# A decoder layer's MLP: the first product in sevens for all pairs, two of each seven made early and kept in DRAM, the second product in sevens for every other pair

## The chip, the cores and the metric

The kernel runs on one core of a Trainium2 chip. The metric is the device time of one execution in microseconds (us). The core has five engines with instruction queues of their own: TensorE (PE in the profile, with its weight loads as PEld), VectorE (DVE), ScalarE (ACT), GpSimd (POOL) and SyncE (SP), whose queue here carries the DMA transfers. Each engine works through its queue in order; semaphores make one wait for another. Matmul results go to PSUM, in banks of 128 x 512 fp32; everything else lies in SBUF or in DRAM.

## The reference

One layer: attention and a recurrent mixer in parallel, merged into `h`; then a dense MLP; then a gated embedding. The change concerns the MLP. 1024 tokens, 1024 columns, 4096 hidden columns, all fp32:

```
f = rmsnorm(h, ffn_pre_norm[i])
f = jnp.square(jax.nn.relu(f @ w_ff_in[i])) @ w_ff_out[i]
h = h + rmsnorm(f, ffn_post_norm[i])
```

## The kernel before, in words

**fp32 in three matmuls.** Each fp32 operand is split into a rounded part (hi, by an ACT copy) and the rest (lo, by a DVE or POOL subtraction). `mm3` (line 289) issues hi·hi, hi·lo and lo·hi for each block of 128 rows: lines 292, 294 and 296 of the profile, 128x512 each.

**The order of the work.** A planner written in Python (`Engine`, `Loads`, `Order`) interleaves generators by estimated times; it decides in which order instructions are written. All ACT, DVE and POOL calls go through line 113 and all transfers through line 132, so the profile tells them apart by tile names. From the MLP on, SP's queue is in the order in which the code issues the transfers.

**First product.** The hidden columns are cut into 32 blocks of 128 (`j`), two to a pair `p` (NP = 16 pairs). For each block and each half of the tokens, `ff1_half` (1450) sums 8 x 3 = 24 matmuls into a fresh bank (`zbank`, 341; tile z, operands f and wh/wl), and `ff1_evac` (1454) applies ReLU and the square into `raw_h` (tile hr). That makes 64 x 24 = 1536 matmuls.

**Second product.** It goes pair by pair: 1024 tokens x 256 hidden columns times 256 x 1024 weights. As 2 x 2 blocks this takes eight block products; pairs 0 to 14 do it in seven (Strassen-Winograd), at the price of sums of operands. `operands` (1499) makes the sums on POOL (tiles sum, ws), `prep` (1530) splits them two products ahead (tile duo; ACT, DVE, POOL), `product` (1540) does 4 banks x 3 matmuls (tile bk) and adds each bank into the running totals (tile tot, DVE) while later products of a chain go on accumulating in the same four banks (tags s1 to m1). The order of the seven is MUL = (2, 1, 6, 5, 3, 7, 4). Pair 15 is done plainly with 96 matmuls (`ff2_last`, 1649; tiles lw, lh). That makes 15 x 84 + 96 = 1356 matmuls.

**How they interleave.** `ff1(j)` (1583) puts one product of the second kind, for the pair before, behind every 12 matmuls of the first. `load_w2` (1480) loads the second product's weights (w2r). `part` (1564) takes weights of later stages through the engines piece by piece: load (gp), ACT copy, DVE subtraction (gpl), two stores to DRAM (pke, pkl, pkg). The first product's weights come by `wload` (313): load (wr), ACT copy (wh), POOL subtraction (wl).

**Before the MLP,** `mixed` (1409) norms the token tiles i = 0 to 7 and `put_T` (1391) transposes and splits each into f. Tiles 0 to 3 are the first half of the tokens, 4 to 7 the second.

## Time and profile before

| | |
|---|---|
| Median of 3 runs | 1774.25 us (1773.64 to 1776.46) |
| Profiled execution, its own time | 1773.19 us |
| Its span, first to last instruction | 1771.4 us |
| Mean granted TensorE clock | 0.999 |
| PE busy | 98% |
| DVE, ACT, POOL busy | 57%, 41%, 38% |
| DMA traffic | 175.51 MB, mean 99 GB/s |

How to read the profile's lines: a group is "line, engine, operation, out<-in, shape, xcount | busy us, mean ns of one | idle of the engine just before them, and who ended it". A timeline row is start, length, engine, line, operation, and in brackets the idle before it with its releaser. A wait is "who <- for whom: us in total, times, longest". A DMA row is "out<-in, queue, xcount, KB each, us from issue to landing".

### The profile page before, as it was taken

The numbers are of one execution on the slowest core, as the hardware profiler recorded it, in microseconds if no ns is written. First come the engines' busy times: TensorE is split into PE (matmuls) and PEld (weight loads), VectorE is DVE, ScalarE is ACT, GpSimd is POOL, SyncE is SP. The second block draws the span as 40 slices with busy tenths as digits, with TensorE's granted clock in tenths as the row PEclk, the third lists the DMA queues.
The fourth block names the chain that finished last, engine by engine and source line by source line (L and its number), as shares of the span: only waits on it lengthen the run. The fifth ranks groups of instructions, "written<-read, shape, count | busy, mean of one in ns | idle before, by whom it ended". The sixth has DMA issues, their size and how long they took to land.

```text
span 1771.4 us, 25935 instructions
## 1 busy us (share of the span) xinstructions
PE 1743.8 (98%) x10192; PEld 1423.4 (80%) x10192; DVE 1017.1 (57%) x1834; ACT 732.3 (41%) x1315; POOL 670.5 (38%) x423
## 2 busy tenths in 40 slices
PE   9999989999999999999999999999999999999998
PEld 8787877878877777778888878888788888888887
DVE  6289777776534233353735466665666566556643
ACT  5824343432344343542434434343334334333454
POOL 1344131231232323332230266666665566652311
PEclk9999999999999999999999999999999999999999
DMA  4621121212332222333524132332232232305611
GB/s 163 211 95 37 49 78 47 98 43 96 86 134 84 60 60 72 110 111 135 201 96 139 64 113 95 94 115 87 92 118 91 84 95 90 123 9 179 214 48 48
DMA packets 67132, 175.51 MB, mean 99 GB/s; under 512 B 7745, under 2 KB 8129, under 8 KB 66498
## 3 DMA queue, kind: packets, MB, share of 16 engines
q1 hardware_dynamic: 67010, 173.86, 29.6%
q8 instruction: 80, 1.31, 0.3%
q14 instruction: 42, 0.34, 0.1%
HBM read 125.20 MB, written 41.94 MB: 94 GB/s over the span
## 4 chain that ended last, share of the span: by engine, by line
PE 82%; DVE 5%; DMA 5%; ACT 3%; POOL 2%; issue 2%; SPq 0%; DVEq 0%; ACTq 0%; POOLq 0%
PE z L294 18%; PE z L296 18%; PE z L292 18%; PE bk L292 6%; PE bk L294 5%; PE bk L296 5%; PE sc L275 1%; DVE xy L113 1%; PE y L275 1%; PE po L275 1%; PE pt L283 1%; PE A L275 1%; PE wr L275 1%; PE fq L275 1%; POOL wl L113 1%
## 5 line engine op out<-in xcount | busy, mean ns | idle before, releaser
L113 POOL TENSOR_TENSOR wl<-wr,wh 128x1024 fp32r<-128x1024 f32 (+1 forms) x87 | 208.0, 2392 | 431.4 <-ACT wh L113 412.2
L113 DVE TENSOR_TENSOR tot<-tot,bk 128x512 f32<-128x512 f32 x420 | 272.7, 682 | 129.9 <-PE bk L296 129.7
L292 PE MATMUL z<-uh,wh 128*128 128x512 f32 (+1 forms) x800 | 312.3, 390 | 5.5 <-ACT part L113 3.0
L296 PE MATMUL z<-uh,wl 128*128 128x512 f32 (+1 forms) x800 | 312.6, 391 | 2.7 <-POOL wl L113 2.7
L294 PE MATMUL z<-ul,wh 128*128 128x512 f32 (+1 forms) x800 | 313.6, 392 | 1.3 <-DVE ul L113 1.3
L292 PE MATMUL z<-f,wh 128*128 128x512 f32 x496 | 193.2, 389 | 0.3 <-ACT f L113 0.3
L294 PE MATMUL z<-f,wh 128*128 128x512 f32 x496 | 193.1, 389 | 0.2 <-DVE f L113 0.2
L296 PE MATMUL z<-f,wl 128*128 128x512 f32 x496 | 193.0, 389 | 0.0
L292 PEld LDWEIGHTS z<-uh,wh 128*128 128x128 f32 x800 | 151.1, 189 | 36.2 <-ACT part L113 3.5
L296 PEld LDWEIGHTS z<-uh,wl 128*128 128x128 f32 x800 | 151.0, 189 | 34.1 <-POOL wl L113 4.0
L294 PEld LDWEIGHTS z<-ul,wh 128*128 128x128 f32 x800 | 151.2, 189 | 32.3 <-issue 3.6
L292 PE MATMUL bk<-duo 128*128 128x512 f32 x420 | 164.3, 391 | 4.0 <-DVE tot L113 3.9
L294 PE MATMUL bk<-duo 128*128 128x512 f32 x420 | 163.5, 389 | 0.0
L296 PE MATMUL bk<-duo 128*128 128x512 f32 x420 | 163.5, 389 | 0.0
L113 ACT ACTIVATE wh<-wr 128x1024 fp32r<-128x1024 f32 (+1 forms) x87 | 90.3, 1038 | 119.0 <-PE z L294 89.8
L113 POOL TENSOR_TENSOR duo<-w2r,duo 128x512 fp32r<-128x512 f32 x45 | 66.7, 1483 | 166.0 <-ACT duo L113 166.0
L113 POOL TENSOR_TENSOR duo<-ws,duo 128x512 fp32r<-128x512 f32 x60 | 81.0, 1350 | 122.3 <-ACT duo L113 119.0
L292 PEld LDWEIGHTS z<-f,wh 128*128 128x128 f32 x496 | 93.1, 188 | 20.0 <-ACT f L113 0.5
L294 PEld LDWEIGHTS z<-f,wh 128*128 128x128 f32 x496 | 93.1, 188 | 19.8 <-DVE f L113 0.5
L296 PEld LDWEIGHTS z<-f,wl 128*128 128x128 f32 x496 | 93.1, 188 | 19.2
L292 PEld LDWEIGHTS bk<-duo 128*128 128x128 f32 x420 | 78.8, 188 | 23.7 <-DVE tot L113 7.0
L296 PEld LDWEIGHTS bk<-duo 128*128 128x128 f32 x420 | 78.8, 188 | 16.4
(312 smaller groups left out, 3203.5 us busy)
## 6 DMA issues: line engine op xcount, KB each, us to landing
wr<-in_wz_dram SPq DMA_DIRECT2D x48, 512.0 KB, 3.7
wr<-in_wff_dram SPq DMA_DIRECT2D x31, 512.0 KB, 3.6
w2r<-in_w_ff_dram SPq DMA_DIRECT2D x30, 512.0 KB, 4.2
xt<-in_x_dram SPq DMA_DIRECT2D x16, 512.0 KB, 4.3
gscr<-gst SPq DMA_DIRECT2D x32, 256.0 KB, 2.0
g<-gscr SPq DMA_DIRECT2D x16, 512.0 KB, 4.2
wpg<-pkg SPq DMA_DIRECT2D x16, 512.0 KB, 6.7
sw<-qk SPq DMA_DIRECT2D x48, 128.0 KB, 2.3
```

The source lines that it names most:

```text
L113: return f(*a, **kw)
L275: PE.matmul(out_, a, b, start=start, stop=stop)
L283: PE.transpose(out_, a, ident if idn is None else idn)
L292: PE.matmul(ps, ah, bh, start=start and i == 0, stop=False, skip_group_check=not start)
L294: PE.matmul(ps, ah, bl, start=False, stop=False, skip_group_check=not start)
L296: PE.matmul(ps, al, bh, start=False, stop=i == n - 1, skip_group_check=not start)
```

## The change

**First product in sevens.** Per pair it is now a 2 x 2 block product too: the input columns in two halves times the pair's two blocks of 128, and the two token halves. `put_f` takes the place of `put_T` and builds seven operands F[1] to F[7]; those that need the second half of the tokens get sums on DVE and POOL at tiles 4 to 7. Each product is 12 matmuls: 84 per pair, 16 x 84 = 1344 in all. Products 1 and 2 need only the first half of the tokens: `early` makes them for all 16 pairs (32 products, 384 matmuls) while tiles 4 to 7 are still normed, and stores them to DRAM (p1scr, cscr). The other five (SEQ = 6, 7, 4, 5, 3) are made by `first`, which `chunks` cuts into pieces of three matmuls; `take` loads the early results into `raw_h`, three times product 1 and once the finished block. After each of the five, DVE adds the bank into a block of `raw_h`. Products 6, 7, 4 accumulate in one bank, 5 and 3 in another.

**Second product.** Even pairs keep their sevens (`seven`; 8 x 84), odd pairs are done plainly (`plain`; 7 x 96), pair 15 as before (96): 1440 matmuls. The weight sums of an even pair p are made by `w2_sums` during the plain phase of pair p − 1, split, stored to DRAM (bs) and loaded again by `prep`. Some SBUF areas (tags) are assigned anew; `rooms` says which tags hold the operands of a phase, and `w2_sums` stages its splits in two of them.

```diff
+    def put_f(srcs, i):
+        ts = slice((i % 4) * 128, (i % 4) * 128 + 128)
+        if i == 4:
+            for n, p, h in ((3, 0, 0), (7, 1, 0), (5, 0, 1), (6, 1, 1)):
+                t = mtile("hl"[p], h, [128, 2, 4, 512], "f", F32R)
+                F[n] = t[:, 0], t[:, 1]
+            F[4] = [rtile([128, 4, 512], "f", tag, F32R) for tag in ("AR0", "AR1")]
...
+        G.tensor_tensor(c, c, at(1, 0), OP.subtract)
+        G.tensor_tensor(c, c, at(1, 1), OP.subtract)
+        G.tensor_tensor(t4, at(2, 0), t2, OP.subtract)
+        G.tensor_tensor(t4, t4, at(2, 1), OP.add)
+        for n, x, eng in ((7, d, V), (6, t2, V), (5, c, G), (4, t4, G)):
+            S.activation(at(n, 0), x, AF.Copy)
+            eng.tensor_tensor(at(n, 1), x, at(n, 0), OP.subtract)
...
-    def ff1_half(ps, hi, lo, h):
-        return mm3(ps, [(hi[:, k * 128:(k + 1) * 128], lo[:, k * 128:(k + 1) * 128],
-                         fT[0][h][:, k, slice(0, 512)], fT[1][h][:, k, slice(0, 512)]) for k in range(KT)])
-    def ff1_evac(ps, j, h):
-        p, x = j // 2, 2 * (j % 2) + h
-        if p not in raw_h:
...
+    SEQ = (6, 7, 4, 5, 3)
+    A_, W1, w1 = {}, {}, []
+    p1_scr, c_scr = ([dram.tile([128, 512], F32, name=f"{n}scr{p}") for p in range(NP)] for n in ("p1", "c"))
+    bs_scr = {(p, i): dram.tile([128, 2, 512], F32, name=f"bs{p}_{i}") for p in range(0, NP - 1, 2) for i in (6, 5, 7, 4)}
...
+    prods = []
+    for p in range(0, NP, 2):
+        prods += [(p, 1), (p + 1, 1), (p, 2), (p + 1, 2)]
+    NA = len(prods)
+    prods += [(p, i) for p in range(NP) for i in SEQ]
+    def a_raw(k):
+        if k < NA:
+            p, i = prods[k]
+            SY.dma_start(A_["raw"][:, k % 4], quarter(p, i - 1))
+    def w1_split(k):
+        if k >= len(prods):
+            return
+        p, i = prods[k]
+        src = A_["raw"][:, k % 4] if k < NA else W1[{6: "s2", 7: "21", 4: "22", 5: "s1", 3: "12"}[i]]
+        w = w1[k % 3]
+        S.activation(w[:, 0], src, AF.Copy)
+        (V if k < NA and k % 4 == 3 else G).tensor_tensor(w[:, 1], src, w[:, 0], OP.subtract)
...
+    def w1_mm(k, ps, start):
+        w, f = w1[k % 3], F[prods[k][1]]
+        return mm3(ps, [(w[:, 0, c * 128:c * 128 + 128], w[:, 1, c * 128:c * 128 + 128], f[0][:, c, :], f[1][:, c, :])
+                        for c in range(4)], start)
+    def early(k):
+        p, i = prods[k]
+        a_raw(k + 4)
+        w1_split(k + 2)
+        if k == 0:
+            A_["out"] = rtile([128, 4, 512], "pa", "UV")
+        if i == 1:
+            A_[p] = bank()
+        ps = A_[p]
+        yield from w1_mm(k, ps, i == 1)
+        dst = A_["out"][:, k % 4]
+        if i == 1:
+            S.activation(dst, ps, AF.Copy)
+        else:
+            S.activation(dst, ps, AF.Relu)
+            S.activation(dst, dst, AF.Square)
+        SY.dma_start((p1_scr if i == 1 else c_scr)[p], dst)
...
+    def first(k):
+        p, i = prods[k]
+        n = SEQ.index(i)
+        if n in (3, 4):
+            w1_sum(p + 1, n - 1)
+        w1_split(k + 2)
+        if n == 2:
+            w1_sum(p + 1, 1)
+        if n == 0:
+            w1_sum(p, 4)
+            w1_raw(p + 1, "21", "11")
+        if n == 1:
+            w1_raw(p + 1, "22")
+        if n == 3:
+            w1_raw(p + 1, "12")
+        if n in (0, 3):
+            W1["ps"] = zbank()
+        ps = W1["ps"]
+        yield from w1_mm(k, ps, n in (0, 3))
+        x = raw_h[p][:, {6: 1, 7: 3, 4: 2, 5: 3, 3: 1}[i]]
+        V.tensor_tensor(x, x, ps, OP.add)
+        if i in (4, 5, 3):
+            S.activation(x, x, AF.Relu)
+            S.activation(x, x, AF.Square)
...
+    def chunks(n):
+        while Y["n"] < n:
+            if Y["g"] is None:
+                Y["g"] = first(Y["k"])
+                Y["k"] += 1
+            for _ in range(3):
+                yield next(Y["g"])
+            Y["n"] += 1
+            if Y["n"] % 4 == 0:
+                for _ in Y["g"]:
+                    pass
+                Y["g"] = None
+    def take(p):
+        if p < NP:
             raw_h[p] = rtile([128, 4, 512], "hr", ("BK", "UV")[p % 2])
-        f1 = rtile([128, 512], "f1", "gst")
-        S.activation(f1, ps, AF.Relu)
-        S.activation(raw_h[p][:, x], f1, AF.Square)
-        if x == 3 and p == NP - 1:
-            last_split(1, (1,), ())
+            for x, src in ((1, p1_scr), (3, p1_scr), (2, p1_scr), (0, c_scr)):
+                SY.dma_start(raw_h[p][:, x], src[p])
+    def mlp():
+        last["turn"] = tc.manual_schedule(engines={mybir.EngineType.SP})
+        last["turn"].__enter__()
+        while sch.t < t_f.get(3, 1e9):
+            yield 0.0
+        for k in range(NA):
+            beside(k)
+            yield from early(k)
+        while sch.t < t_f.get(7, 1e9):
+            yield 0.0
+        yield from chunks(16)
+        take(1)
+        yield from chunks(20)
+        prep(0)
+        prep(1)
+        for p in range(1, NP):
+            Y["n"] = 0
+            e = p - 1
+            if e % 2 == 0:
+                for x in range(7):
+                    yield from chunks((20 * x + 20 + 3) // 7)
+                    yield from seven(items.index((e, x)))
+                    if x == 0:
+                        load_w2(p)
+                    if x == 4:
+                        take(p + 1)
+                    if p == NP - 1:
+                        if x in (1, 2, 5):
+                            e_weights((1, 2, 5).index(x))
+                        if x == 5:
+                            last_split(0, (0,), (0,))
+                            last_split(1, (0, 1), (1,))
+                continue
+            for u in range(8):
+                yield from chunks((20 * u + 20 + 3) // 8)
+                if u == 0:
+                    load_w2(p)
+                yield from plain(items.index((e, u // 2)), u % 2)
+                if u == 1:
+                    take(p + 1)
+                if 0 < u < 6 + 1:
+                    w2_sums(p, u - 1)
+                part(2 * p - 4 + u // 2, u % 2)
...
+    def rooms(e):
+        r = (("Ep", "En"), ("a", "px"), ("kk", "v"))
+        return (r[1], r[0], r[2]) if e // 2 % 2 else r
...
+        x = n - 1 - (n > 3)
+        d = split2((t2, t1, t1, t2)[x], rooms(p)[1][x % 2], G)
+        SY.dma_start(bs_scr[p, (6, 5, 7, 4)[x]], d.bitcast(F32))
...
-        a, b = operands(p, i)
-        duo[n] = (split2(a, ("Ep", "En", "a")[n % 3], V),
-                  split2(b, ("kk", "MP", "px")[n % 3], G))
+        e, x = items[n]
+        if e % 2 == 0:
+            i, room = MUL[x], rooms(e)[x % 3]
+            a = split2(operand(e, i), room[0], G)
+            if i in (2, 1, 3):
+                b = split2(w_blocks(e)[{2: 2, 1: 0, 3: 3}[i]], room[1], G)
+            else:
+                b = rtile([128, 2, 512], "duo", room[1], F32R)
+                SY.dma_start(b.bitcast(F32), bs_scr[e, i])
+            duo[n] = a, b
+            return
+        m, c = x // 2, x % 2
+        if c == 0:
+            room = rooms(e - 1)[1 + m]
+            duo[e, m] = [split2(raw_h[e][:, 2 * j + m], room[j], V) for j in range(2)]
+        if m == 0:
+            if c == 0:
+                ops["w"] = [rtile([128, 2, 1024], "ws", t, F32R) for t in ("BT", "BK2")]
+            hi, lo = ops["w"]
+            for j in range(2):
+                o = (slice(None), j, halves[c])
+                S.activation(hi[o], raw_w[e][j][:, halves[c]], AF.Copy)
+                G.tensor_tensor(lo[o], raw_w[e][j][:, halves[c]], hi[o], OP.subtract)
+    XB = ("s1", "s2", "s3", "m0", "m1")
...
+    def plain(n, part):
+        e, x = items[n]
+        if part == 0:
+            prep(n + 2)
+        m, c = x // 2, x % 2
+        a, (hi, lo) = duo[e, m], ops["w"]
+        for t in (2 * part, 2 * part + 1):
+            ts = slice(t * 128, t * 128 + 128)
+            ps = bank(XB)
+            yield from mm3(ps, [(a[j][:, 0, ts], a[j][:, 1, ts], hi[:, j, halves[c]], lo[:, j, halves[c]])
+                                for j in range(2)])
+            V.tensor_tensor(tot[m][c][:, t], tot[m][c][:, t], ps, OP.add)
...
+    def part(u, x):
+        if u >= 2 * len(GP):
             return
         dst, k, src = GP[u // 2]
         c = halves[u % 2]
         if x == 0:
-            gp["t"] = rtile([128, 2, 512], "gp", "v", F32R)
-            SY.dma_start(gp["t"][:, 0].bitcast(F32), src[:, c] if len(src.shape) == 2 else src[:, u % 2])
+            gp["t"] = rtile([128, 512], "gp", "gst")
+            SY.dma_start(gp["t"], src[:, c] if len(src.shape) == 2 else src[:, u % 2])
             return
-        raw, hi = gp["t"][:, 0].bitcast(F32), gp["t"][:, 1]
-        lo = rtile([128, 512], "gpl", "yc", F32R)
+        raw, hi = gp["t"], rtile([128, 512], "gph", "gst", F32R)
+        lo = raw.bitcast(F32R)
         S.activation(hi, raw, AF.Copy)
         V.tensor_tensor(lo, raw, hi, OP.subtract)
         SY.dma_start(dst[:, k, 0, c], hi.bitcast(F32))
         SY.dma_start(dst[:, k, 1, c], lo.bitcast(F32))
...
-    def ff1(j):
-        def body(hi, lo):
-            p = j // 2
-            if j == 3:
-                last["turn"] = tc.manual_schedule(engines={mybir.EngineType.SP})
-                last["turn"].__enter__()
-            muls = iter(range(7 * p - 7 + 4 * (j % 2), 7 * p - 7 + (7 if j % 2 else 4)))
-            for h in range(0 if j > 2 else 1, 2):
-                ps = zbank()
-                g = ff1_half(ps, hi, lo, h)
-                for k in range(2):
-                    for _ in range(12):
-                        yield next(g)
-                    if k:
-                        for _ in g:
-                            pass
-                        ff1_evac(ps, j, h)
-                    for n in [x for _ in range(1 if j > 2 else 2) for x in (next(muls, None),) if x is not None]:
-                        yield from product(n)
-                        part(n)
-                        if n % 7 == 1:
-                            load_w2(n // 7 + 1)
-                        if n in E_LOADS:
-                            e_weights(E_LOADS.index(n))
-                        if n == 7 * NP - 10:
-                            last_split(0, (0, 1), (0,))
-                        if n == 7 * NP - 9:
-                            last_split(1, (0,), (1,))
-        sch.add(body, lambda: wload(wff1[j]) if j > 2 else third())
```

In the new order, PE comes to this place in the even phase of pair 4: the boundary from product 6 (operands f_8509, weights wh_8379) to product 7 (f_8507, wh_8380), both in the bank z_10575.

```order
L292 MATMUL z_10575<-f_8509,wh_8379 128x512
L294 MATMUL z_10575<-f_8509,wh_8379 128x512
L296 MATMUL z_10575<-f_8509,wh_8379 128x512
L292 MATMUL z_10575<-f_8507,wh_8380 128x512 [waits DVE_49,Activation_49]
L294 MATMUL z_10575<-f_8507,wh_8380 128x512
L296 MATMUL z_10575<-f_8507,wh_8380 128x512 [waits Pool_49]
```

Here product 7 follows product 6 on the bank with nothing between them, and waits for DVE. On the same engine before, a first-product bank (z_12027, operands f10 and f11) ends and a second-product bank (bk_11999, product with operands duo_11996) goes on:

```order
L292 MATMUL z_12027<-f10_8329,wh_11788 128x512
L294 MATMUL z_12027<-f11_8330,wh_11788 128x512
L296 MATMUL z_12027<-f10_8329,wl_11789 128x512
L292 MATMUL bk_11999<-duo_11996,duo_11993 128x512 [waits DVE_49,Activation_49]
L294 MATMUL bk_11999<-duo_11996,duo_11993 128x512 [waits Pool_49]
L296 MATMUL bk_11999<-duo_11996,duo_11993 128x512
```

There other matmuls stood between a bank's uses; now a bank is used again at once.

SP's queue at the start of the even phase of pair 4: bs4_6, bs4_5, bs4_7 and bs4_4 are the four stored weight sums, duo_10592 is the third product's weight operand, gp and gph a piece of a later weight, pke its place in DRAM.

```order
L132 DMA bs4_4_655<-duo_10531 128x1024 [waits DMAHW2_49,Pool_49]
L132 DMA gp_10535<-in_pT_dram 128x512 [waits DMAHW4_49,DMAHW0_49]
L132 DMA pke_118<-gph_10565 128x512 [waits Activation_49]
L132 DMA pke_118<-gp_10535 128x512 [waits DMAHW5_49,DVE_49]
L132 DMA wr_8382<-in_wff1_dram 128x512 [waits DMAHW6_49]
L132 DMA wr_8382<-in_wff1_dram 128x512 [waits DMAHW7_49]
L132 DMA duo_10592<-bs4_6_652 128x1024 [waits PE_49]
```

The load that PE needs (the last row) has moved into a queue behind a store that waits for POOL and two that wait for ACT and DVE. ACT's own queue at the same place (duo_10531 is the staged sum, duo_10674 the next operand, in the buffer that the store above reads):

```order
L113 ACTIVATE duo_10531<-sum_10349 128x512 [waits PE_49]
L113 ACTIVATE duo_10671<-sum_10669 128x512 [waits DVE_49]
L113 ACTIVATE wh_8380<-wr_8383 128x512 [waits PE_49,Pool_49]
L113 ACTIVATE duo_10674<-w2r_10287 128x512 [waits DMAHW2_49,Pool_49]
L113 ACTIVATE gph_10565<-gp_10535 128x512 [waits DMAHW3_49,DMAHW1_49]
```

The copy of the staged sum waits for PE, and the later weight's copy gph stands behind an operand that waits for the store. In the kernel before, none of these steps was there: weight sums stayed on chip, and SP's queue held only loads of weights and stores of `part`:

```order
L132 DMA wr_11926<-in_wff1_dram 128x1024 [waits DMAHW2_49,Pool_49]
L132 DMA pkg_117<-gp_11909 128x512
L132 DMA pkg_117<-gpl_12019 128x512 [waits DMAHW4_49,DVE_49]
L132 DMA w2r_12024<-in_w_ff2_dram 128x1024 [waits Pool_49]
L132 DMA w2r_12024<-in_w_ff2_dram 128x1024 [waits DMAHW6_49]
```

So operands of second products came from an engine in SBUF, and come now in part from DRAM.

More of the change, by code (lines that the diff above doesn't have):

```diff
@@ L1380, in layer @@
     gn = {}
-    fT = [[None, None], [None, None]]
+    F = {}
     def ss2(srcs, jks):
@@ new lines, in w1_raw @@
+    def w1_raw(p, *names):
+        for n in names:
+            if p < NP:
+                SY.dma_start(W1[n], quarter(p, ("11", "12", "21", "22").index(n)))
+    prods = []
[15 more added lines that the diff above has]
+        (V if k < NA and k % 4 == 3 else G).tensor_tensor(w[:, 1], src, w[:, 0], OP.subtract)
@@ L1464, in last_split, with mlp_ahead @@
+    def mlp_ahead(x):
+        if x == 0:
+            w1_tiles()
+            for k in range(4):
+                a_raw(k)
+        else:
+            w1_split(0)
+            w1_split(1)
     def last_split(k, hs, ws):
@@ L1538, in layer, with seven @@
+    XB = ("s1", "s2", "s3", "m0", "m1")
     chain = [None] * 4
-    def product(n):
-        p, i = n // 7, MUL[n % 7]
+    def seven(n):
+        p, x = items[n]
+        i = MUL[x]
         prep(n + 2)
@@ L1683, in last_weights @@
     def last_weights():
-        pg = pieces(GA, "wpg", F32R)
-        P["wpg"] = [[Split(pg[4 * p:4 * p + 4]), mtile("hl"[p], 0, [128, KT, 512], "wpg", F32R)]
-                    for p in range(2)]
+        P["wpg"] = [[mtile("hl"[p], 1 - c, [128, KT, 512], "wpg", F32R) for c in range(2)] for p in range(2)]
         P["g3"] = rtile([128, D], "g3", "v")
@@ L1813, in layer @@
         out_1(i)
-    ff1_first()
-    for j in range(2, 2 * NP):
-        ff1(j)
+    sch.add(mlp)
     for i in range(8):
```

197 lines of the change are left out of this document (104 added, 93 removed).

## The prediction, made before the changed kernel had run

> **What bounds the kernel now.** I read the list of cores first, then the page's busy times and its chain, then the windows by stage, the groups by shape, the waits and last the timeline.
>
> ```profile
> core 0: 1771.4 us, clock 0.999
> PE 1743.8 (98%) x10192; PEld 1423.4 (80%) x10192; DVE 1017.1 (57%) x1834; ACT 732.3 (41%) x1315; POOL 670.5 (38%) x423
> PE 82%; DVE 5%; DMA 5%; ACT 3%; POOL 2%; issue 2%; SPq 0%; DVEq 0%; ACTq 0%; POOLq 0%
> ```
>
> TensorE is busy in 98% of the span at full clock, and 82% of the chain that ended last are matmuls. The MLP lies between about 1000 and 1640 us; in the windows (span, then PE, PEld, DVE, ACT, POOL busy, clock, DMA share, GB/s) that stretch is this row:
>
> ```profile
> 1000.00:1640.00 640.00, 635.49 (x2802) 523.40 (x2801) 385.66 (x572) 247.02 (x409) 379.75 (x252) 1.00 0.30 97
> ```
>
> PE idles 4.5 of 640 us there, POOL is busy 59%, DVE 60%, ACT 39%, and the DMA engines are at 30%. So only matmuls count, as long as none of them waits. Their spacing comes from two starts, eleven matmuls apart:
>
> ```profile
> 1013.42 0.39 PE L292 MATMUL z<-f,w 128*128 128x512 f32 x1
> 1015.92 0.39 PE L296 MATMUL z<-f,w 128*128 128x512 f32 x1
> ```
>
> (1015.92 − 1013.42) / 11 = 0.227 us each; the 0.39 shown is one matmul's own length, which overlaps the next. And PE waits for almost nobody; these are the two largest entries of the waits on PE, whole program (total, times, longest):
>
> ```profile
> PE bk L292 <- DVE tot L113: 4.2, 5, 1.7
> PE z L292 <- ACT part L113: 3.0, 1, 3.0
> ```
>
> No transfer stands in that list inside the MLP: every product today works on operands that an engine made on chip long before.
>
> **Part by part.**
>
> *Matmuls.* Of the first product 64 × 24 = 1536 matmuls become 16 × 84 = 1344; of the second 15 × 84 + 96 = 1356 become 8 × 84 + 8 × 96 = 1440. Net −108, × 0.227 = **−24.5 us**, all on PE, which is the path. That is the whole gain.
>
> *A bank that is read between two products.* Of the five later products of a pair, 6, 7 and 4 share one PSUM bank and 5, 3 another. After each, DVE adds the bank into a stored sum, and the next product goes on accumulating in that same bank. So its first matmul cannot start before that add has read the bank. The places are 6→7, 7→4 and 5→3: three per pair, 48 in all. In the new order the matmul that waits stands directly behind the last one that DVE waits for: a round trip with nothing of PE's inside. Before, each half of a column block had a bank of its own. The trip's price is in the timeline: a last matmul and the DVE add released by it, then a DVE group and the PE matmul that it released, with the next start.
>
> ```profile
> 1147.40 0.39 PE L296 MATMUL bk<-duo 128*128 128x512 f32 x1
> 1147.83 2.73 DVE L113 TENSOR_TENSOR tot<-tot,bk 128x512 f32<-128x512 f32 x4 [0.23 <-PE bk L296]
> 1020.86 1.88 DVE L113 COPY tot<-bk 128x512 f32<-128x512 f32 x3
> 1021.60 0.50 PE L292 MATMUL bk<-duo 128*128 128x512 f32 x1 [1.21 <-DVE tot L113]
> 1021.93 0.39 PE L294 MATMUL bk<-duo 128*128 128x512 f32 x1
> ```
>
> 0.39 until the matmul's end, 0.04 to DVE's start, 2.73/4 = 0.68 for the add, about 0.05 back to PE (the first of the three copies ends near 1021.5, PE starts at 1021.60), less the 0.227 that would pass anyway: 0.93. After such a wait the next start follows after 0.33 instead of 0.227, so +0.10: 1.03 us. × 48 = 49. At the 5→3 boundaries of the eight odd pairs, two DVE subtractions for operands stand in DVE's queue between PE's end and the add:
>
> ```profile
> L113 DVE TENSOR_TENSOR duo<-hr,duo 128x512 fp32r<-128x512 f32 x45 | 40.6, 901 | 0.4 <-ACT duo L113 0.4
> L113 DVE TENSOR_TENSOR gpl<-gp 128x512 fp32r<-128x512 f32 x28 | 25.6, 916 | 62.5 <-ACT gp L113 62.4
> ```
>
> Part of 2 × 0.90 shows, I take 1.2: + 8 × 1.2 = 10. **+59 us.** Lower end 48 × 0.93 = 45. Upper end: all of the 1.8 shows, 8 × 0.6 = 5 more, and the split of a later weight (the second row) sits in DVE's queue too and waits for ACT and a load, 62.5/28 = 2.2 us each today; one boundary in each of eight pairs behind one such wait is 18: 59 + 5 + 18 = 82.
>
> *Weight sums that go through DRAM.* The weight sums of an even pair are made in the odd phase before it, stored, and loaded again as operands. The last of the four sums is staged in the buffer that product number two of the even pair still reads. From there the new order gives one chain, in each of the seven even phases that an odd one precedes:
>
> 1. the last matmul of the second product ends; ACT's copy of the sum;
> 2. POOL's subtraction; SP's store, in whose queue everything later stands;
> 3. ACT's copy of the next operand, into the buffer that the store must have left;
> 4. behind it on ACT the copy of a later weight, then DVE's subtraction of it;
> 5. SP, held by these two, issues their stores, two loads of first-product weights and, as the fifth, the load of the sum that the third product needs;
> 6. the load lands; PE goes on.
>
> The rows that price it:
>
> ```profile
> L113 ACT ACTIVATE duo<-ws 128x512 fp32r<-128x512 f32 x60 | 37.2, 620 | 54.7 <-PE bk L296 53.2 <-POOL ws L113 1.5
> L113 POOL TENSOR_TENSOR duo<-ws,duo 128x512 fp32r<-128x512 f32 x60 | 81.0, 1350 | 122.3 <-ACT duo L113 119.0 <-PE bk L296 3.2
> L113 ACT ACTIVATE gp<-gp 128x512 fp32r<-128x512 f32 x28 | 17.7, 631 | 81.0 <-DMA gp<-in_w_pleg_dram 45.1 <-DMA gp<-in_w_ple_dram 11.9 <-DMA gp<-in_w_ff_dram 11.4
> bvscr<-a SPq DMA_DIRECT2D x4, 512.0 KB, 2.8
> w2r<-in_w_ff_dram SPq DMA_DIRECT2D x30, 512.0 KB, 4.2
> gscr<-gst SPq DMA_DIRECT2D x32, 256.0 KB, 2.0
> wpg<-pkg SPq DMA_DIRECT2D x16, 512.0 KB, 6.7
> 1137.27 0.43 SPq L132 DMA_DIRECT2D pke<-gp  x1
> 1137.78 0.38 SPq L132 DMA_DIRECT2D pke<-gpl  x1
> ```
>
> 0.62 (ACT) + 1.35 (POOL) + 2.8 (a 512 KB store; `bvscr<-a` is the only row of that kind) + 0.62 + 0.63 (ACT: an operand, a later weight) + 0.92 (DVE, quoted above) + 1.5 (four issues at about 0.4 before the load's own) + 4.2 (a 512 KB load) = 12.6 us. PE has meanwhile nine matmuls, 9 × 0.227 = 2.0, and one of the boundaries above, 1.0. So PE stands for 9.6 us, × 7 = **+67 us**. Low: the store at 2.0 (`gscr<-gst`, half its size) and 1.1 off for steps that overlap: 7.7 × 7 = 54. High: the load at 6.7 and the store 2.8 longer when transfers crowd: 14.9 × 7 = 104. Nothing in before covers this, and a gain is excluded, since a wait for a buffer cannot shorten anything.
>
> *The loads behind it.* The next sum is loaded behind another 1.8 MB on SP's queue and wanted 1.2 products later. What the DMA engines can carry is in one row:
>
> ```profile
> 15.00:20.00 5.00, 5.00 (x45) 5.00 (x45) 3.96 (x8) 2.33 (x6) 0.12 (x1) 1.00 1.04 393
> ```
>
> 1.8 MB at 393 GB/s is 4.6 us after the first load, against 21 matmuls, 4.8 us: nearly covered. I take 1 us × 7 = **+7** (0 to 21: from all covered to 3 us each).
>
> *The start.* For the second half of the tokens, twelve POOL and DVE sums and splits per token tile are added, while the early products want weight splits from POOL as well. Where PE comes to wait for POOL, I price the place at one POOL step, the 1.35 quoted above; I count some seven, 9.5, less the 4.5 of idle that the MLP has today (its places are gone): **+5** (0 to 10). The last pair's weights are loaded later by one queue position per phase: **+1.5** (0 to 3).
>
> *The clock.* The only stretch at the end without matmuls:
>
> ```profile
> 1765.00:1771.40 6.40, 0.00 (x0) 0.00 (x0) 3.17 (x9) 1.27 (x6) 0.72 (x1) 0.88 0.22 82
> ```
>
> The granted clock is 0.88 over 6.4 us without a matmul: about a quarter of it, 1.5 us, at half speed. An idle of 9.6 us exceeds that, so the clock will have fallen when PE resumes, and the first matmuls take up to twice as long. How long it stays low no row of before shows; a stretch of matmuls as long as the fall took to come, 6.4 − 1.5 = 4.9 us, bounds the loss at 4.9/2 = 2.4 per stall, 17 in all. Taken: half, **+8** (0 to 17).
>
> [...]
>
> *POOL as the bound.* It takes on more sums and splits; its steps last between these two:
>
> ```profile
> L113 POOL TENSOR_TENSOR ws<-w2r 128x512 f32<-128x512 f32 x30 | 47.0, 1569 | 11.2 <-PE tp L283 5.5 <-DMA w2r<-in_w_ff_dram 3.0 <-PE bk L296 0.8
> L113 POOL TENSOR_TENSOR sum<-sum,hr 128x512 f32<-128x512 f32 x15 | 19.3, 1289 | 1.2
> ```
>
> One even and one odd phase together have 84 + 96 + 120 = 300 matmuls, 300 × 0.227 = 68 us, and about 40 POOL steps by the order, 40 × 1.4 = 56 us (63 at 1.57). POOL comes closer to PE but stays under it: 0.
>
> Sum on the profiled execution. It took 1773.2 us, span 1771.4, and is 1.06 below the median, 1774.25. 1773.2 − 24.5 + 59 + 67 + 7 + 5 + 1.5 + 8 = 1896; beside the median 1897.
>
> **The rivals.**
>
> *The chain is covered.* If the store and the copies of step 4 are out of the way in time, because the engines get to them earlier than the wait for the buffer lets me believe, PE sees only the boundaries: 1773.2 − 24.5 + 59 + 5 + 1 = 1814. For it: DMA is at 30%. Against it: the wait on the second product is written into the instruction, and all after it is in order. 0.10.
>
> *The boundaries are covered.* If the accumulation need not wait for the add, as today's PE waits on DVE (4.2 us, 5 times) might suggest, only the chain is left: 1897 − 59 = 1838. Against it: today 9 to 21 other matmuls lie between a bank's last matmul and its next. 0.05.
>
> *Not slower.* This is one mechanism: semaphore waits that were long satisfied when PE reaches them. A wait in the order names only the engine. If each of those at the boundaries and at the loads is for an earlier step of that engine, PE streams on and the 108 matmuls are the whole of it: 1774.25 − 24.5 + 5 = 1755. It decides as soon as the new waits cost less than 24.5 in sum, which is 0.5 us per boundary with no stall at the loads. Against it: the add reads the very bank that the next matmul writes. 0.03.
>
> *Worse than my bounds:* 0.02, with one more stall of the chain's kind that I did not find.
>
> **How the numbers follow.** The forecast has 0.80; its time is the sum, 1897. Its own range from the lower ends: 1774.25 − 24.5 + 45 + 54 = 1849, and from the upper ends 1774.25 − 24.5 + 82 + 104 + 21 + 10 + 3 + 17 = 1987. Not all terms go one way together: I cut the top to 1960, since the two large ones share transfers only in part, and take in the second rival at 1838 below. Range 1836 to 1960. What can be told from no change is 0.2%, 3.5 us. All cases but "not slower" lie above that: slower 0.96, faster 0.03, same 0.01 (the "not slower" case with its waits only partly there).
>
> **What would show it.** Right: about 2784 matmuls of 128x512 in the two products; in the waits PE on first-product matmuls for DVE, about 48 times and 1 us each; PE on second-product matmuls for a DMA of the stored sums, seven times near 10 us; seven dips in the clock; PE's share down to about 92%. The steps fail one by one if the boundary waits are rare or longer than 1.5 us, or if the stalls for the loads are under 5 or over 15 us. The whole is wrong if PE is still busy in 97% of the span, or if the time is under 1800.

## The result, and the profile after

The changed kernel takes 1981.29 us, the median of four runs (1977.88 to 1983.99), against 1775.36 us for the kernel before beside it (four runs, 1773.64 to 1778.71): a ratio of 1.1156, 95% interval 1.1129 to 1.1184. It is slower, as forecast, but by 206 us and not by the 123 of the forecast (1897 − 1774.25), and outside the range, whose top was 1960. The profiled execution took 1983.99 us with a span of 1982.2. These are the lines of the changed kernel that answer to the first ones of before: from the list of cores,

```profile
core 0: 1982.2 us, clock 0.959
```

and from the page the busy times and the clock in 40 slices.

```profile
PE 1780.9 (90%) x10084; PEld 1430.5 (72%) x10084; DVE 1043.7 (53%) x1801; ACT 765.0 (39%) x1377; POOL 753.8 (38%) x530
...
PEclk9999999999999999999989998889898989898999
```

PE has 108 matmuls fewer, as said (10192 − 10084), but its busy time rose, from 1743.8 to 1780.9 us. That splits the 210.8 us between the spans (1982.2 − 1771.4) exactly: −24.5 for the 108 matmuls; + 61.6 because the others kept PE busy longer (1780.9 − 1743.8 + 24.5); + 173.7 of idle (1982.2 − 1780.9 = 201.3, against 1771.4 − 1743.8 = 27.6). The waits on PE say whom the idle is for:

```profile
PE bk L292 <- DMA duo<-bs: 77.2, 7, 11.8
PE z L292 <- DVE hr L113: 77.2, 48, 6.3
PE bk L292 <- ACT pa L113: 8.8, 4, 5.1
PE bk L296 <- DVE wh L113: 4.5, 2, 4.0
...
PE bk L296 <- POOL wh L113: 1.8, 1, 1.8
```

The two predicted waits stand on top, seven and 48 times, at the places that were named; the other rows shown are waits of the early products. This is the chain through DRAM at the even phase of pair 4, in the timeline of the changed kernel:

```profile
1322.93 1.15 ACT L113 ACTIVATE duo<-sum 128x512 fp32r<-128x512 f32 x2 [4.71 <-PE bk L296]
...
1323.64 2.52 POOL L113 TENSOR_TENSOR duo<-sum,duo 128x512 fp32r<-128x512 f32 x2 [3.33 <-ACT duo L113]
...
1324.95 0.32 SPq L132 DMA_DIRECT2D bs<-duo  x1
...
1327.90 0.63 ACT L113 ACTIVATE duo<-w2r 128x512 fp32r<-128x512 f32 x1 [3.15 <-DMA bs<-duo]
1328.52 0.63 ACT L113 ACTIVATE gph<-gp 128x512 fp32r<-128x512 f32 x1
...
1329.18 1.24 DVE L113 TENSOR_TENSOR gp<-gp,gph 128x512 fp32r<-128x512 f32 x1 [4.20 <-ACT gph L113]
1330.45 0.32 SPq L132 DMA_DIRECT2D pke<-gp  x1
1330.83 0.97 SPq L132 DMA_DIRECT2D wr<-in_wff_dram  x2
1331.84 0.43 SPq L132 DMA_DIRECT2D duo<-bs  x1
...
1337.73 0.77 PE L292 MATMUL bk<-duo 128*128 128x512 f32 x1 [11.66 <-DMA duo<-bs]
```

Each step is there in the order of the prediction: the copy after PE, POOL, the store, ACT freed by the store (3.15 us of waiting), the later weight, its stores, two loads, and only then the load that PE needs. PE goes on 5.9 us after that load's issue (1337.73 − 1331.84), with 277 GB/s passing at the time (below), where the sum had 4.2; in six of the seven phases it is 5.1 to 6.1 us, in the last 3.8. The last row's 0.77 shows what comes next. Windows of the same place (span, then PE, PEld, DVE, ACT, POOL busy, clock, DMA share, GB/s):

```profile
1328.00:1330.00 2.00, 0.00 (x0) 0.00 (x0) 0.82 (x1) 1.15 (x2) 1.27 (x1) 0.96 0.01 4
1330.00:1336.00 6.00, 0.00 (x0) 0.00 (x0) 0.42 (x1) 0.00 (x0) 0.00 (x0) 0.50 0.87 277
...
1338.00:1340.00 2.00, 2.00 (x6) 1.54 (x6) 0.62 (x1) 1.11 (x2) 0.41 (x1) 0.50 1.05 411
1340.00:1342.00 2.00, 2.00 (x6) 1.63 (x5) 0.82 (x3) 1.19 (x3) 2.00 (x2) 0.50 0.21 83
1342.00:1344.00 2.00, 2.00 (x7) 1.54 (x7) 1.32 (x2) 0.63 (x1) 2.00 (x3) 0.63 0.00 0
1344.00:1346.00 2.00, 2.00 (x11) 1.62 (x10) 0.50 (x1) 0.00 (x0) 2.00 (x3) 1.00 0.87 311
```

The clock falls just before 1330, some 3.8 us after the last matmul, and stays at 0.50 until about 1343.4, that is for 5.7 us after PE has resumed: six or seven matmuls in 2 us, where the full-rate window in the last row has eleven records. By the lengths of the matmuls in the timeline the half rate lasts 2.7 to 5.7 us behind the seven stalls (6 to 13 matmuls); this is the longest.

Of the 48 boundaries, the shortest waits are like the last row here. The first two rows are a long one of another kind, at the 5→3 boundary of an odd pair; the rows between are a long one of an odd phase, with what led up to it:

```profile
1254.70 3.13 DVE L113 TENSOR_TENSOR duo<-hr,duo 128x512 fp32r<-128x512 f32 x2
...
1258.48 0.80 PE L292 MATMUL z<-f,wh 128*128 128x512 f32 x1 [3.18 <-DVE hr L113]
...
1377.98 0.63 ACT L113 ACTIVATE duo<-sum 128x512 fp32r<-128x512 f32 x1 [8.45 <-DMA bs<-duo]
...
1379.90 0.63 ACT L113 ACTIVATE gph<-gp 128x512 fp32r<-128x512 f32 x1 [1.29 <-DMA gp<-in_w_ff_dram]
...
1380.56 0.69 DVE L113 TENSOR_TENSOR gp<-gp,gph 128x512 fp32r<-128x512 f32 x1 [5.29 <-ACT gph L113]
...
1381.17 1.28 DVE L113 TENSOR_TENSOR tot<-tot,bk 128x512 f32<-128x512 f32 x2
...
1382.36 0.68 DVE L113 TENSOR_TENSOR hr<-hr,z 128x512 f32<-128x512 f32 x1
...
1383.19 0.47 PE L292 MATMUL z<-f,wh 128*128 128x512 f32 x1 [3.89 <-DVE hr L113]
...
1399.55 0.47 PE L292 MATMUL z<-f,wh 128*128 128x512 f32 x1 [0.87 <-DVE hr L113]
```

A wait of 0.87 is the bare round trip of the prediction: 0.87 + 0.39 − 0.227 = 1.03 us lost. The prediction had 0.93 for this and reached 1.03 only with 0.10 for the slow restart, which comes on top here too (the next two starts follow after 0.30 and 0.24 instead of 0.227: 0.09), so the trip costs 1.12. The difference is the way back from DVE to PE, 0.15 us (an add that starts at 1324.29 and takes 0.69 lets PE go at 1325.13) and not 0.05.

All 48 at 0.87 would be 41.8 us of idle. The timeline of DVE ahead of each longer wait sorts the other 35.4 (77.2 − 41.8): 17.9 at nine boundaries behind the later weight's subtraction, as in the middle rows (three of the nine have one subtraction for an operand in front as well); 11.4 at the eight 5→3 boundaries behind the two subtractions for operands, as in the first two; 5.7 at two boundaries of the first even phase, one of them 6.26 us long, where DVE's own sums wait for POOL; 0.3 in small change. In the middle rows ACT stands for a store of an earlier staged sum, the later weight's copy stands behind it on ACT, DVE's subtraction behind that, and behind DVE's subtraction the two totals and the add that PE waits for.

### The profile page after: what moved, and what is told of

Same layout as the page of the kernel before. It is cut to its first block, busy times and chain, and to the rows that moved or that the text cites. A ratio compares the mean times of both kernels' runs of the same rounds, so it can differ in the third digit from the quotient of the medians.

```text
span 1982.2 us, 26323 instructions
## 1 busy us (share of the span) xinstructions
PE 1780.9 (90%) x10084; PEld 1430.5 (72%) x10084; DVE 1043.7 (53%) x1801; ACT 765.0 (39%) x1377; POOL 753.8 (38%) x530
## 3 DMA queue, kind: packets, MB, share of 16 engines
q8 instruction: 79, 1.29, 0.3%
## 4 chain that ended last, share of the span: by engine, by line
PE 64%; DVE 12%; DMA 10%; ACT 5%; POOL 4%; issue 3%; SPq 1%; DVEq 0%; ACTq 0%; POOLq 0%
PE z L292 12%; PE z L296 12%; PE z L294 12%; PE bk L292 5%; PE bk L296 5%; PE bk L294 5%; DVE tot L113 2%; DMA duo<-bs 2%; SPq L132 1%; DMA g<-gscr 1%; DVE duo L113 1%; DMA gp<-in_w_pleg_dram 1%; DVE hr L113 1%; DMA bs<-duo 1%; DMA pkg<-gph 1%
## 5 line engine op out<-in xcount | busy, mean ns | idle before, releaser
L113 DVE TENSOR_TENSOR tot<-tot,bk 128x512 f32<-128x512 f32 x336 | 226.4, 686 | 219.0 <-PE bk L296 218.5
L113 POOL TENSOR_TENSOR wl<-wr,wh 128x1024 fp32r<-128x1024 f32 (+1 forms) x56 | 132.5, 2368 | 420.4 <-ACT wh L113 401.2
L292 PE MATMUL bk<-duo 128*128 128x512 f32 x224 | 98.0, 437 | 77.2 <-DMA duo<-bs 77.2
L292 PE MATMUL z<-f,wh 128*128 128x512 f32 x212 | 87.8, 414 | 52.7 <-DVE hr L113 52.7
L113 ACT ACTIVATE wh<-wr 128x1024 fp32r<-128x1024 f32 (+2 forms) x89 | 78.1, 878 | 138.2 <-PE z L294 103.8
L113 POOL TENSOR_TENSOR duo<-sum,duo 128x512 fp32r<-128x512 f32 x64 | 84.6, 1331 | 87.7 <-ACT duo L113 87.7
L292 PEld LDWEIGHTS bk<-duo 128*128 128x128 f32 x224 | 47.8, 213 | 90.6 <-issue 80.1
L113 ACT ACTIVATE duo<-sum 128x512 fp32r<-128x512 f32 x64 | 38.9, 628 | 157.2 <-PE bk L296 72.5
L294 PE MATMUL bk<-duo 128*128 128x512 f32 x224 | 95.6, 427 | 0.0
L296 PE MATMUL bk<-duo 128*128 128x512 f32 x224 | 95.0, 424 | 0.0
L292 PEld LDWEIGHTS z<-f,wh 128*128 128x128 f32 x212 | 40.8, 192 | 73.2 <-ACT wh L113 20.7
L292 PE MATMUL bk<-ws,duo 128*128 128x512 f32 x224 | 89.5, 400 | 0.0
L294 PE MATMUL bk<-ws,duo 128*128 128x512 f32 x224 | 88.7, 396 | 0.0
L296 PE MATMUL bk<-ws,duo 128*128 128x512 f32 x224 | 88.5, 395 | 0.0
L296 PE MATMUL z<-f,wh 128*128 128x512 f32 x212 | 84.8, 400 | 0.0
L294 PE MATMUL z<-f,wh 128*128 128x512 f32 x212 | 84.6, 399 | 0.0
```

The lines of the kernel that those rows point to most:

```text
L113: return f(*a, **kw)
L292: PE.matmul(ps, ah, bh, start=start and i == 0, stop=False, skip_group_check=not start)
L294: PE.matmul(ps, ah, bl, start=False, stop=False, skip_group_check=not start)
L296: PE.matmul(ps, al, bh, start=False, stop=i == n - 1, skip_group_check=not start)
```

## The experiments

Theories: (A) the boundaries, the chain, the start and the clock each cost what PE is seen to wait there, and removing one removes its time; (B) something wider is the bound (transfers, POOL or DVE as a whole), and a wait that is removed comes back elsewhere.

**1. The weight sums a step earlier.** They are made ahead of the plain product of the same step, not behind it.

```diff
+                if 0 < u < 6 + 1:
+                    w2_sums(p, u - 1)
                 yield from plain(items.index((e, u // 2)), u % 2)
...
-                if 0 < u < 6 + 1:
-                    w2_sums(p, u - 1)
```

> The weight sums of an even pair are made ahead of the plain product of the same step, so the last one's staging no longer waits for the second product of the next phase; nothing else changes. Stall theory: the seven waits of PE for the stored sums (77.2 us) go, and with them the half-rate matmuls behind each, about 13 x 0.2 = 2.6 us, 18 us in all: about 1981 - 77 - 18 = 1886 us; the 48 waits for DVE stay near 77 us. Rival (crowded transfers: the loads of the sums are slow because 242 MB pass instead of 175): the loads still come late, PE still waits 3 us or more at each, and the time stays above 1930.

1899.05 us (two runs, 1896.28 to 1901.82; ratio to before 1.0662 to 1.0725): 82 us less than the changed kernel, not 95. No wait for the stored sums is left, so the loads are quick enough when their chain is gone, and crowded transfers are not the cause. Its largest waits on PE:

```profile
PE z L292 <- DVE hr L113: 77.7, 47, 7.5
PE bk L292 <- ACT pa L113: 9.1, 4, 5.2
```

**2. A bank for each of the five products.** The sums between them go through SBUF.

```diff
-        if n in (0, 3):
-            W1["ps"] = zbank()
-        ps = W1["ps"]
-        yield from w1_mm(k, ps, n in (0, 3))
-        x = raw_h[p][:, {6: 1, 7: 3, 4: 2, 5: 3, 3: 1}[i]]
-        V.tensor_tensor(x, x, ps, OP.add)
+        ps = zbank()
+        yield from w1_mm(k, ps, True)
+        h = raw_h[p]
+        x = h[:, {6: 1, 7: 3, 4: 2, 5: 3, 3: 1}[i]]
+        V.tensor_tensor(x, h[:, {6: 1, 7: 1, 4: 3, 5: 3, 3: 1}[i]], ps, OP.add)
+        if i == 5:
+            V.tensor_tensor(h[:, 1], h[:, 1], ps, OP.add)
...
-            for x, src in ((1, p1_scr), (3, p1_scr), (2, p1_scr), (0, c_scr)):
+            for x, src in ((1, p1_scr), (0, c_scr)):
```

> Each of the five later products gets a bank of its own; the sums between them are made by DVE in SBUF (one more DVE add per pair, two loads fewer). The chain through DRAM stays. Stall theory: the 48 waits for DVE (77.2 us idle, 85 us against the pace) go, the seven waits for stored sums stay near 11 us each, dips of the clock stay only behind those: about 1981 - 85 - 15 = 1881 us. Rival (DVE is the bound in the plain phases, since later weights' splits and waits for stores block its queue): the waits move to the first-product banks or the totals and at least 30 us of them stay, time above 1910.

1891.66 us (two runs, 1890.92 to 1892.40; 1.0625 to 1.0678): 90 us less. No boundary wait is left and DVE's long queue delays nobody; the stalls of the chain are a little longer, since the boundary ahead of each of the seven is gone and PE gets there earlier (7 × 1.12 = 8, an estimate):

```profile
PE bk L292 <- DMA duo<-bs: 85.7, 7, 13.3
PE bk L292 <- ACT pa L113: 8.8, 4, 5.1
PE bk L292 <- issue: 6.4, 1, 6.4
```

**3. Both.**

> Both edits together. Stall theory: only the matmuls' own saving of 24.5 us and the waits at the start (about 20 us with their clock) are left, against 7.6 us of idle that the kernel before has there: 1775 - 24.5 + 20 - 7 = about 1764 us, clock above 0.99. Rival (DMA traffic or POOL as a new bound): PE waits elsewhere for more than 25 us in sum and the time stays at or above 1780.

1805.84 us (four runs, 1801.96 to 1809.26; 1.0144 to 1.0199). The two edits add up: 93 us for the banks on top of the first edit, 86 for the sums on top of the second. But the stall theory's 1764 is missed by 42 us. Time and waits are on the rival's side (PE idles 62.5 us, 1801.9 − 1739.4, against 27.6 before), yet transfers or POOL as the bound is not what the odd and even phases show: they run nearly without waits, clock 0.99. And still the kernel is 30 us slower than before. Its windows, and that of the kernel before for the first stretch:

```profile
980.00:1110.00 130.00, 109.45 (x449) 85.34 (x449) 52.91 (x59) 66.37 (x130) 85.89 (x61) 0.92 0.48 168
1110.00:1640.00 530.00, 517.92 (x2256) 423.69 (x2256) 356.32 (x505) 210.96 (x361) 401.71 (x300) 0.99 0.51 179
```

```profile
980.00:1110.00 130.00, 127.68 (x570) 104.18 (x569) 76.21 (x119) 52.62 (x95) 73.09 (x49) 1.00 0.26 88
```

In the 130 us of the early products PE does 449 matmuls on record, before it did 570. The 121 missing ones are 121 × 0.227 = 27 us of lost time: the start, for which the prediction had 5.

**4. Matmuls that nobody reads, in the stalls of the changed kernel.** F[3] is an operand of the first product, the bank is a free one.

```diff
+                    if x == 2 and e > 0:
+                        keep = zbank()
+                        for _ in range(48):
+                            PE.matmul(keep, F[3][0][:, 0, 0:128], F[3][0][:, 0, :], start=True, stop=True)
                     yield from seven(items.index((e, x)))
```

> 48 matmuls of 128x512 whose result nobody reads (extra work, 10.9 us of PE time) are put in front of the third product of each even phase with a stall, into a free bank; all waits stay as they are. Clock theory: PE idles hardly at all in those seven places, so the clock holds and the matmuls behind run at full rate: each stall costs what it did, but the half rate behind it, about 2.6 us, goes: 1981 - 18 = about 1963 us or a little more if the filler outlasts a stall. Rival (slow matmuls come from contention with the transfers of that place): the fillers and the matmuls behind them are slow as well, the clock is no different, and the time is 1981 or above.

1985.91 us (two runs, 1983.65 to 1988.17), against 1981.29: nothing gained, a miss. The clock did hold, 0.976 instead of 0.959 over the whole, and the matmuls behind a filled stall run at full rate: from the seven stalls to the next boundary waits none takes over 0.55 us, where the changed kernel has 70. The same place as above:

```profile
1326.47 11.05 PE L1640 MATMUL z<-f 128*128 128x512 f32 x48
1338.86 0.47 PE L292 MATMUL bk<-duo 128*128 128x512 f32 x1 [1.34 <-DMA duo<-bs]
...
1356.12 0.80 PE L292 MATMUL z<-f,wh 128*128 128x512 f32 x1 [3.75 <-DVE hr L113]
```

```profile
1337.73 0.77 PE L292 MATMUL bk<-duo 128*128 128x512 f32 x1 [11.66 <-DMA duo<-bs]
...
1355.19 0.50 PE L292 MATMUL z<-f,wh 128*128 128x512 f32 x1 [1.56 <-DVE hr L113]
```

The second fence is the changed kernel. From the stall's end to the end of the next boundary wait it is 17.3 us with the filler and 17.5 without (1356.12 − 1338.86, 1355.19 − 1337.73): what PE won by its clock it waited away at the boundary, 3.75 instead of 1.56 us, since that end is set by DVE's queue. And that longer wait drops the clock in its turn: seven matmuls behind the 3.75 us take over 0.55 us, none behind the 1.56. Over all seven places this is a part of the answer: from resuming to the end of the next boundary wait PE needs 119.3 us in sum instead of 124.3, so 5 us are kept; but the stalls with the filler in them last 85.3 us in sum instead of 80.0, counted from the start of the last matmul of the kernel ahead to that of the first behind, and that takes the 5 us back. Why they last longer is not shown.

**5. The later weights' subtraction on POOL,** on top of the first edit.

```diff
-        V.tensor_tensor(lo, raw, hi, OP.subtract)
+        G.tensor_tensor(lo, raw, hi, OP.subtract)
```

> On top of the sums made earlier (the kernel of about 1899 us): the subtraction of each later weight's piece runs on POOL instead of DVE. Theory: about 36 of the 77.7 us that PE waits for DVE at the 47 or 48 boundaries come from DVE being held behind that subtraction, which waits for ACT, a load and a store; then the waits fall towards 47 x 0.87 = 41 us plus some 10 for the plain operands' splits, the half-rate matmuls behind them mostly go (10 us), and the time is about 1899 - 27 - 10 = 1862 us. Rival (the plain operands' splits on DVE make the excess): waits stay above 65 us, time above 1890.

1873.03 us (two runs, 1872.15 to 1873.90): 26 us less, where 37 were expected. The boundary waits fall by 14 us, though not as far as 51, and PE's busy time by 22 (1774.1 to 1752.0), since fewer matmuls run at half rate (granted clock 0.986 instead of 0.975; in the last 420 us 26 matmuls over 0.55 us instead of 48); a part of both comes back as idle elsewhere:

```profile
PE z L292 <- DVE hr L113: 63.7, 45, 7.4
```

So that subtraction in DVE's queue is one cause of the long boundaries and worth 26 us. The longer waits that are left stand, by the timeline, behind the two subtractions for operands, behind DVE's sums of hr that wait for POOL, and in the first even phase (7.39 us); no run takes these out one by one.

**6. The start, first attempt,** on top of both edits: an own bank for the early second product, and more weight splits on DVE.

```diff
-        if i == 1:
-            A_[p] = bank()
-        ps = A_[p]
-        yield from w1_mm(k, ps, i == 1)
+        ps = bank()
+        yield from w1_mm(k, ps, True)
...
-            S.activation(dst, ps, AF.Relu)
+            V.tensor_tensor(dst, A_["out"][:, k % 4 - 2], ps, OP.add)
+            S.activation(dst, dst, AF.Relu)
...
-        (V if k < NA and k % 4 == 3 else G).tensor_tensor(w[:, 1], src, w[:, 0], OP.subtract)
+        (V if k < NA and (k % 4 == 3 or k > 12 and k % 2) else G).tensor_tensor(w[:, 1], src, w[:, 0], OP.subtract)
```

> On top of both edits (the kernel of about 1806 us): the early second product gets a bank of its own and DVE adds the first to it, and DVE takes every second weight split from the 13th early product on. Theory: of the loss at the start (about 28 us of waits and 10 of half-rate matmuls between 980 and 1110 us), what waits for the evacuation (ACT pa, 10 us) and for POOL's splits (6 us) goes, with some of the clock: about 1806 - 20 = 1786 us. Rival (the engines are simply overloaded while the tiles of the second half are normed): the waits move to other operands and the time stays above 1800.

1811.88 us (four runs, 1807.68 to 1813.38), against 1805.84: no gain. The waits for the evacuation are gone and stand at the weights instead, the longest being 7.45 us for DVE's split.

**7. Fillers without boundaries:** the filler of run 4 on top of run 2.

> On top of own banks alone (the kernel of about 1892 us, with the seven stalls for stored sums but no boundary waits): 48 matmuls that nobody reads fill each stall. Theory (half-rate matmuls cost their time unless a later wait takes it back): here no boundary wait follows that could, so the 133 slow matmuls fall to about 60 and the time to about 1892 - 15 = 1877 us. Rival (the time between two stalls is set by the chain of other engines, so PE's pace behind a stall does not matter): the next stall grows by what is saved and the time stays within 4 us of 1892.

1883.28 us (two runs, 1882.21 to 1884.36) against 1891.66: 8.4 us less, clock 0.989 instead of 0.965. Half of what was expected, but a gain: with no boundary behind the stall nothing takes it back. This is about the net price of the clock behind seven stalls.

**8. The start, second attempt,** on top of run 6: none of the first 13 weight splits on DVE, and the second product's weights for pair 1 loaded a step earlier.

```diff
-        (V if k < NA and (k % 4 == 3 or k > 12 and k % 2) else G).tensor_tensor(w[:, 1], src, w[:, 0], OP.subtract)
+        (V if 12 < k < NA and k % 2 else G).tensor_tensor(w[:, 1], src, w[:, 0], OP.subtract)
...
         prep(1)
+        load_w2(1)
...
-                    if x == 0:
+                    if x == 0 and p > 1:
                         load_w2(p)
```

> On top of the kernel of about 1812 us: DVE takes no weight split among the first 13 early products (POOL does), and the second product's weights of pair 1 are loaded a step earlier. Theory (DVE is overloaded between 1000 and 1010 us, its sums there take 1.76 us instead of 0.69 while POOL works): the wait of 7.45 us for DVE's weight split goes, and the one stall of 6.4 us in the first even phase: about 1812 - 7 - 6 = 1799 us. Rival (POOL is then late in its place): the time stays within 5 us of 1812.

1805.77 us (four runs, 1799.25 to 1807.72), 6 us less than run 6 and level with run 3. The stall in the first even phase has shrunk from 6.4 to 1.2 us, as expected; the start has not gained, for the waits moved on to ACT and POOL.

**9. The sums left out,** on top of both edits.

```diff
-        V.tensor_tensor(t2, d, at(1, 0), OP.add)
...
-        G.tensor_tensor(t4, t4, at(2, 1), OP.add)
-        for n, x, eng in ((7, d, V), (6, t2, V), (5, c, G), (4, t4, G)):
+        for n, x, eng in ((7, d, V), (6, d, V), (5, c, G), (4, d, G)):
```

> On top of both edits (the kernel of about 1806 us): the six sums per token tile that build the operands of products 4 to 6 are left out (two on DVE, four on POOL; the splits are made of what the sums would have started from, so the numbers are not the layer's). Theory (these sums, made while the tiles of the second half are normed, are what the early products wait behind): of the loss of about 38 us between 980 and 1110 us some 15 to 20 go: about 1788 us. Rival (weight splits and evacuations alone are too much): the loss stays above 30 us and the time above 1799.

1790.76 us (two runs, 1790.32 to 1791.20; 1.0059 to 1.0104): 15 us less than run 3. PE gets through 546 matmuls in the first stretch where run 3 had 449:

```profile
980.00:1110.00 130.00, 123.56 (x546) 99.39 (x545) 42.30 (x65) 77.34 (x152) 75.72 (x57) 0.99 0.56 191
```

So most of the loss at the start, 97 of the 121 missing matmuls, is made by those six sums per token tile on DVE and POOL; of these 22 us the whole kernel keeps 15. They can't be left out, and even without them the kernel is not below the one before. No version that was run beats it.

## Why the prediction was wrong

The direction, the two mechanisms, their places and their counts were right: 48 waits for DVE and seven for a stored sum. The sizes were not. Runs 1 to 3 split the 206 us into parts: −24.5 + 54 (what run 3 keeps: 1805.84 − 1776.14 = 29.7, + 24.5) + 93 (run 1 to run 3) + 82 (changed kernel to run 1) = 205. Against the forecast 83 us are missing: 48 of them in what run 3 keeps (54 for 6.5), 34 in the boundaries (93 for 59).

- **Matmuls, −24.5:** right; 10192 − 10084 = 108.
- **The chain, 67, with 7 for the loads behind it and 8 for the clock: 82.** Measured 82 (86 without the boundaries). The steps of the chain were right; that the sum is right to the microsecond is partly luck: 77.2 of idle against 67, mostly because the load took 5.1 to 6.1 us in six phases and not 4.2; nothing for the later loads; and for the clock, where the prediction took half of its upper end, 8.4 us in run 7.
- **The boundaries, 59, at most 82.** Measured 90 and 93 us, by runs 2 and 3. This step failed. The round trip was close, 1.12 for 1.03 us (54 for 49), and so were the subtractions for operands at the 5→3 boundaries (11.4 us of idle for 10). What was mis-sized is the rest of DVE's queue in front of the add: nothing in the sum, and 17.9 us of idle behind the later weight's subtraction and 5.7 in the first even phase in the trace; 54 + 11 + 18 + 6 = 89. I saw the later weight's subtraction there, but priced its wait by the 62.5 us over 28 of before, where nothing delayed ACT, and put it in the upper end only. In the new order ACT waits, as in the rows above, 8.45 us for a store of staged sums first, and everything behind it on ACT and DVE waits along. Run 5 takes that one step out of DVE's queue: 26 us, with the clock that it costs.
- **The start, 5, and 1.5 for the last loads.** Measured 54 with all that is left in run 3, some 27 of it in the 130 us of the early products, 17 between 1110 and 1640 us (2256 matmuls on record in run 3, 2330 before), 6 of these in one stall of the first even phase (run 8); the remaining 10 no run explains, nor is the 1.5 shown by itself. This step failed too, and worst. I counted places where PE waits one deep for POOL and set their sum, 9.5, against idle of before. What the windows show is bursts in which both engines are nearly full. These are the ten us from 1000 on, first in the kernel before, then in the changed one:

```profile
1000.00:1010.00 10.00, 9.47 (x45) 7.46 (x44) 1.38 (x2) 4.74 (x8) 6.06 (x5) 1.00 0.00 0
1000.00:1010.00 10.00, 5.99 (x19) 4.21 (x18) 9.79 (x8) 3.39 (x8) 8.48 (x7) 0.84 0.00 0
```

DVE is busy 9.79 of these 10 us and POOL 8.48, and operands are late; counting single waits could not show that. Over the whole 130 us they are not full (52.9 and 85.9 us in run 3). Adding up the new steps against the time of a token tile might have shown it, as I did for one pair of phases, but not here. Run 9 shows that the six sums make most of it; whether by their number or because some of DVE's sums take longer beside POOL's steps (1.76 instead of 0.69 us, last section) no run separates. Runs 6 and 8 show that two other ways to share out the rest do not cure it.
- **The clock, 8, at most 17.** For the seven stalls it was right in net (run 7). But the changed kernel's PE was busy 61.6 us longer for the same matmuls. 55 waits (7 + 48) and a dozen at the start explain 67 × 0.16 = 11 of it (the end of a matmul that a wait uncovers) and 67 × 0.10 = 7 (the slow restart); about 43 us are left for matmuls at half rate, behind stalls, behind long boundaries, and at the start. The timeline agrees: from 900 us on 193 matmuls take over 0.55 us, none in the kernel before, and 193 × 0.2 = 39 (0.43 from start to start instead of 0.227). I gave the clock to the seven stalls alone. Part of it costs nothing, as run 4 shows: a boundary behind it waits less for it (1.56 instead of 3.75 us in the rows there).
- **The range.** The sum of the upper ends was 1987 and would have held the 1981. I cut it to 1960 because the large terms would not all go one way, and they did not: the chain with its loads and clock came to 82, far below its upper ends (104 + 21 + 17), while the boundaries (90 to 93) and the start lie above theirs (82, and 10 + 3). So 1987 would have held the result by luck, one error covering another. Nor do the terms hang on one cause: runs 1 and 2 take the chain and the boundaries out one by one, and each gives nearly the same with and without the other (82 and 86, 93 and 90).

The 17 rests on 4.9 us of matmuls at half rate: that the clock needs as long to come back as it took to fall was the prediction's estimate, and no run shows it. What the trace shows is 0.50 granted from about 3.8 us into the stall above, and half rate for 2.7 to 5.7 us after PE resumed, behind the seven; with the filler of run 4 none of it. Waits of 2.56 and 1.81 us lost the clock too (last section).

## What to carry to other kernels

Count a bank that is read between two accumulations as a full round trip of the reading engine, here 1.12 us, and then look at what else is in that engine's queue, with the waits that the new order gives it and not those of the old profile. Where a change adds steps to a burst of work, add them up against the burst's length on each engine before counting single waits. Look at a store of a staged operand that stands in one queue with the loads that the bound engine needs: here everything behind it waited along, and making the operand one step earlier took 82 us away.

## What was not expected of the hardware

Short waits were enough to lose the clock, and their length alone does not decide it. The first two rows are from the early products of the changed kernel, the other two are boundaries:

```profile
1083.38 0.50 PE L296 MATMUL bk<-f,wh 128*128 128x512 f32 x1 [1.81 <-POOL wh L113]
...
1084.25 0.63 PE L296 MATMUL bk<-f,wh 128*128 128x512 f32 x1
...
1572.47 0.76 PE L292 MATMUL z<-f,wh 128*128 128x512 f32 x1 [2.56 <-DVE hr L113]
...
1750.56 0.47 PE L292 MATMUL z<-f,wh 128*128 128x512 f32 x1 [2.23 <-DVE hr L113]
```

The first matmul after the 2.56 us takes 0.76 us and its followers 0.63; after 2.23 us it takes 0.47, as after the waits of 0.87, and no slow one follows. After the 1.81 us at the start three matmuls run fast, and then seven take 0.63. After the 3.89 us above (1383.19), too, the first ones were fast and the slow ones came 1.2 us later. What decides, no run shows.

And one group of DVE's sums of two SBUF operands, with POOL at work beside them, took two and a half times as long at the start as those that read PSUM, beside which POOL worked for 0.06 us at most; both groups of the changed kernel between 980 and 1030 us:

```profile
L113 DVE TENSOR_TENSOR t<-t,f 128x512 f32<-128x512 f32 x3 | 5.3, 1755 | 0.0
...
L113 DVE TENSOR_TENSOR f<-tp,f 128x512 fp32r<-128x512 f32 x3 | 2.1, 684 | 0.6 <-ACT f L113 0.6
```

1755 against 684 ns (tp is in PSUM, t and f are in SBUF). Other sums there whose operands are all in SBUF lie between, or a little above (f<-d,f 1400, t<-d,f 1048, f<-t,f 1794). That SBUF operands alone are not slow shows later in the same kernel, in the tile sum, with both operands in SBUF in both rows (shortest, median and longest in ns, first and last start):

```profile
L113 DVE TENSOR_TENSOR sum<-sum,hr x8: 685/686/691, 1128.6 to 1788.2; 128x512 f32<-128x512 f32 x8
L113 DVE TENSOR_TENSOR sum<-hr,sum x8: 1736/1761/1765, 1137.9 to 1794.4; 128x512 f32<-128x512 f32 x8
```

By the timeline no POOL step runs beside any of the first eight, and each of the second eight starts 0.07 to 0.08 us behind the start of a POOL step. The one at 1221.87 takes 1.76 us, the POOL step in front of it 1.29. The adds tot<-tot,bk, which read a bank in PSUM, take 0.67 to 0.69 us with POOL at work beside them for 90% of their length or more (146 adds) and with POOL idle beside them (126). And t<-d,f at 1017.56, in SBUF, starts together with a POOL step of 1.81 us and takes 0.69. What makes the others longer, no run shows.
